# A recurrence's result kept on chip for one token group, and its square roots queued later on ScalarE

## The chip, the cores and the metric

The kernel runs on one core of one Trainium2 chip. The metric is the device time of one execution in microseconds. Before the change the median of three runs is 3213.04 us (3211.27 to 3219.51). The core has a matrix engine (TensorE, PE in the profile; PEld is its weight load), a vector engine (VectorE, DVE), an activation engine (ScalarE, ACT), GpSimd (POOL) and SyncE (SP), which here issues nearly all transfers. Each engine works through its own queue in order and meets the others through semaphores.

## The reference

One step of a hybrid decoder layer over 1024 prompt positions and 8 x 4 sample positions, 1056 rows of width 1024:

```
z  = rmsnorm(x) @ w_in
h  = x + [ rwkv7(z_r) | pool(z_p) ] @ w_out
h  = h + peer(rmsnorm(h))            # 8 heads: two scores of 128 keys, top 16 of each,
                                     # top 16 of the sums, gather of expert rows u and v
h  = h + (p @ w_ple) * sigmoid(rmsnorm(h) @ w_pg)
y  = rmsnorm(h)
```

The change lies in `rwkv7`, 8 heads of 64 with one 64 x 64 state each:

```
s    = s * w_t + (s @ -kk_t) (kk_t a_t)^T + v_t k_t^T ;   out_t = s @ r_t
out  = (out - mean(out)) * rsqrt(var(out) + 64e-5) * lnx_g + lnx_b     # per head and row
y_r  = (out + bonus) * g
```

All eight results are returned: y for both groups and the new shift, state and pooling buffers.

## The kernel before

**Stages.** Phase A projects x and makes the factors of the recurrence. Phase B is the recurrence, cut into 16 chunks of 64 prompt rows plus one for the samples. Phase C works on four token groups, columns 0 to 288, 288 to 544, 544 to 800 and 800 to 1056 (the samples are the first 32): output projection (8 blocks of `w_out`), norm, query projection (16 blocks of `wq`) and key scores. The top-k stage picks experts; for most rows it writes gates into a dense table, by one-hot matmuls or by scatters on GpSimd. Then 128 expert blocks run as dense matmuls, and the last layers follow.

**A chunk** (`bchunk`) is a generator. Each `yield` ends a turn: matmuls into one PSUM bank and a copy or product out of it. The turns are: one for `ltm` (L513), two for `lp` (L522), then an inverse by doubling, whose first copy is L533 and whose levels 1 to 5 have two turns each, a `zp` copy (L539) and a `yx` copy (L547), both on ScalarE; then `kbT` (L555), `vt` and `wn` (L560, L580), `u` (L585), the new state S on DVE (L617, L618), and the output `po`. The last part is called the tail here: head means (L625) and centring (L627) on DVE, four squarings with sums (L631), then `inv_sqrt` (a square root on ScalarE at L186 and a reciprocal on DVE at L187), a turn's end, the scaling (L634), a transposition on TensorE into a PSUM bank, two DVE products and additions into `yo` (L638, L639), and a store of `yo` to `y_d` in memory (L640, on SP). A chunk has 20 turns. Chunk c holds columns 32 + 64c onward, so chunks 8 to 11 are the third group's.

**Order.** `b_stream` keeps up to three chunks alive in three slots; a new one starts six rounds after the last at the earliest, and when a slot is free. A round gives each live chunk one turn. All chunk matmuls share one pool of four PSUM banks. Buffers such as `zp`, `yx` and `kbT` belong to a slot.

`merge` interleaves streams by shares of planned length. In step 1 phase C of the first group runs beside chunks 5 to 7; in step 2 phase C of the second beside chunks 8 to 11 and the top-k of the first; in step 3 phase C of the third beside chunks 12 to 15 and the top-k of the second; in step 4 phase C of the last with the remaining top-k and the first dense blocks. `b_stream` may run up to two chunks ahead of a step. What is traced is then put in order per engine by a planner, which simulates the engines in time and takes the ready instruction that was traced first. `tc.issue_after(l)` binds what is traced in its block to come behind `l` on `l`'s engine, in order alone and without a wait for its end.

**A group's start** (`phase_c`). The tile y is loaded from `y_d` (L720, on SP), then eight pieces of h from `hx_d` (L725), which are bound behind that load. y is split into a high and a low part (L708 on ScalarE, L709 on DVE), and the first `w_out` block follows (matmuls L677 to L679, addition to h at L739). For the two middle groups y lies in a tile `gst` of the pool `gp`, one of two buffers, which the one-hot stage also uses; the others take a tile of the work pool. The query copies on ScalarE are L800. h has one buffer; the last thing that reads it is a store (L776). Scores go to memory (L811) and come back for the top-k (L833).

Of the kernel before, what the change touches and what calls it, by code (L numbers as in the profile page):

```python
# [10 lines left out]
F32 = mybir.dt.float32  # L11
# [4 lines left out]
AF = mybir.ActivationFunctionType  # L16
# [9 lines left out]
HD = 64  # L26
# [14 lines left out]
GROUPS = ((0, 288), (288, 544), (544, 800), (800, 1056))  # L41
# [5 lines left out]
TC = 32  # L47
# [5 lines left out]
EB = 128  # L53
# [12 lines left out]
def body(ctx, tc, io):  # L66
    nc = tc.nc
    mm = nc.tensor.matmul
    TT, STT, TS, ACT = (nc.vector.tensor_tensor, nc.vector.scalar_tensor_tensor, nc.vector.tensor_scalar,
                        nc.scalar.activation)  # L70
# [7 lines left out]
    y_d = dram.tile([128, 4, T], F32, name="y_d")  # L78
# [10 lines left out]
    def v3(ap, n):  # L89
        return ap.rearrange("p (a b) -> p a b", b=n)  # L90
# [15 lines left out]
    leps_t = const.tile([128, 1], F32)  # L106
# [25 lines left out]
    def PS(tag):  # L132
        return pools[tag].tile([128, 512], F32, name="ps", tag="bc" if tag in ("b0", "b1") else tag)
# [51 lines left out]
    def inv_sqrt(out, src, scale, eps):  # L185
        ACT(out, src, AF.Sqrt, bias=eps, scale=scale)  # L186
        nc.vector.reciprocal(out, out)  # L187
# [279 lines left out]
            yield  # L467

    maxn = max(b - a for a, b in GROUPS)
    def bchunk(c, sp=None):  # L470
        smpl = sp is not None
        slot = 1 if smpl else c % NSLOT
        pst = "b0"
        tt = NSMP if smpl else 64
        pos = 0 if smpl else NSMP + 64 * c
# [3 lines left out]
        def wt(name, n, bufs=1):  # L479
            return pb.tile([128, n], F32, name=name, tag=f"{name}{slot}", bufs=bufs)  # L480

        def q4(name, bufs=1):
            return v3(wt(name, 256, bufs), 64)

        def quad(ps):
            return v3(ps[:, :256], 64)
# [4 lines left out]
        def hmm(o, l, r, start, stop):  # L491
            for hs in HS:
                mm(o[hs], l[hs], r[hs], start=start, stop=stop)  # L493

        def pmm(o, l, r, start, stop):
            for p in range(4):
                hmm(o[:, p], l[:, p], r[:, p], start and (start != "one" or p == 0), stop and (stop != "one" or p == 3))

        def turn(o, i):
            for p in range(4):  # L500
                hmm(o[:, p], i[:, p], ident2, True, True)

        f = sp[3] if smpl else pb.tile([128, 28, 64], F32, name="fdc", bufs=NSLOT + 1)
# [4 lines left out]
        ps = PS(pst)  # L508
# [6 lines left out]
        for pp in range(2):  # L515
            ps = PS(pst)
            pv = ps[:, :384].rearrange("m (i q t) -> m i q t", i=2, q=3)
            for i in range(2):
                p = 2 * pp + i
# [6 lines left out]
        yx = wt("yx", 512).rearrange("m (j q t) -> m j q t", j=2, q=4)  # L526
        Y, X = yx[:, 0], yx[:, 1]
        ps = PS(pst)
# [5 lines left out]
        for l in range(1, nlev):  # L534
            ps = PS(pst)
            hmm(ps[:, :256], id16[:, 0, :], id16.rearrange("m q t -> m (q t)"), True, False)
            pmm(quad(ps), ltm[:, l], Y, False, "one")
            zp = q4("zp")
            ACT(zp, quad(ps), AF.Copy)  # L539
            yield  # L540
            ps = PS(pst)
            n = 1 if l == nlev - 1 else 2
            pyx = ps.rearrange("m (j q t) -> m j q t", j=2, q=4)
            pmm(pyx[:, 0], X, zp, True, True)
            if n == 2:
                pmm(pyx[:, 1], zp, X, True, True)
            ACT(yx[:, :n], pyx[:, :n], AF.Copy)  # L547
            yield

        kbT = wt("kbT", 512).rearrange("m (j q t) -> m j q t", j=2, q=4)  # L550
        ps = PS(pst)
# [5 lines left out]
        ps = PS(pst)  # L557
# [41 lines left out]
        if smpl:  # L599
            po = out()  # L600
            for p in range(4):
                ps = PS(pst)
# [26 lines left out]
        s2 = wt("s2", 4)  # L629
        for p in range(4):  # L630
            STT(sq[:, p], cen[:, p], 1.0, cen[:, p], op0=ALU.mult, op1=ALU.mult, accum_out=s2[:, p:p + 1])  # L631
        inv_sqrt(s2, s2, 1.0 / HD, leps_t)
        yield
        TT(cen, cen, s2[:, :, None].to_broadcast([128, 4, 64]), op=ALU.mult)  # L634
        ps = PS(pst)
        turn(quad(ps), cen)
        yo = v3(pb.tile([128, 256], F32, name="yo", tag=f"kbT{slot}"), 64)
        TT(yo, quad(ps), fg, op=ALU.mult)  # L638
        TT(yo, yo, fo, op=ALU.add)  # L639
        nc.sync.dma_start(y_d[:, :, pos:pos + tt], yo[:, :, :tt])  # L640

    wraws = {}

    def wblock(gi, b):
        if b >= C3E and gi == NG - 1:
            hi, lo = esplit(io["wq"][b - KB])
            return [(t[0], t[1]) for t in zip(*[(x[:, :HK], x[:, HK:]) for x in (hi, lo)])]
        out = []
        for i in range(1 if b < KB else 2):
            ks = slice(i * HK, (i + 1) * HK)  # L650
            hi = ws.tile([128, HK, 128], F32R, name="whi", bufs=3)
            lo = ws.tile([128, HK, 128], F32R, name="wlo", bufs=3)
            if gi == 0:
                if b < 4:
                    raw = tk.tile([128, HK, 128], F32, name="wraw", tag="oh", bufs=2)
                else:
                    if b % 4 == 0 and i == 0:
                        wraws[0] = gp.tile([128, EB, TC], F32, name="gst", bufs=2)
                    raw = v3(wraws[0][:, 16 * (b % 4 if b < KB else 2 * (b % 4) + i):][:, :16].rearrange("p a b -> p (a b)"), 128)
                nc.sync.dma_start(raw, (io["w_out"][b] if b < KB else io["wq"][b - KB])[:, ks, :])  # L660
                ACT(hi, raw, AF.Copy)
                TT(lo, raw, hi.bitcast(F32), op=ALU.subtract)
                nc.sync.dma_start(wc_d[b, :, 0, ks, :], hi.bitcast(F32))
                nc.sync.dma_start(wc_d[b, :, 1, ks, :], lo.bitcast(F32))
            else:
                nc.sync.dma_start(hi.bitcast(F32), wc_d[b, :, 0, ks, :])
                nc.sync.dma_start(lo.bitcast(F32), wc_d[b, :, 1, ks, :])
            out.append((hi, lo))
        return out
# [23 lines left out]
    def segs(gi):  # L693
        c0, c1 = GROUPS[gi]
        if c0 == 0:
            return ((0, NP, NSMP), (NSMP, 0, c1 - NSMP))
        return ((0, c0 - NSMP, c1 - c0),)

    def tiles_of(gi):
        n = GROUPS[gi][1] - GROUPS[gi][0]  # L700
        return [(t, min(128, n - t)) for t in range(0, n, 128)]

    def phase_c(gi):
        c0, c1 = GROUPS[gi]
        n = c1 - c0
# [6 lines left out]
            ACT(hi, h[:, b, :n], AF.Copy, scale=vec(V_G2, b))  # L712
            STT(lo, h[:, b, :n], vec(V_G2, b), hi.bitcast(F32), op0=ALU.mult, op1=ALU.subtract)

        if 0 < gi < NG - 1:
            y = gp.tile([128, EB, TC], F32, name="gst", bufs=2).rearrange("p a b -> p (a b)")
            y = v3(y[:, :4 * maxn], maxn)
        else:
            y = work.tile([128, 4, maxn], F32, name="y", tag="yp")
        ly = nc.sync.dma_start(y[:, :, :n], y_d[:, :, c0:c1]).ins  # L720
        h = work.tile([128, KB, maxn], F32, name="h")
        with tc.issue_after(ly):
            for b in range(KB):
                for d, s, L in segs(gi):
                    nc.sync.dma_start(h[:, b, d:d + L], hx_d[:, b, s:s + L])  # L725
# [9 lines left out]
        for b in range(KB):  # L735
            w = wblock(gi, b)
            ps = PS("b2")
# [17 lines left out]
        a, b = max(c0, GA), min(c1, GB)  # L755
# [26 lines left out]
        for t0, m in tiles_of(gi):  # L782
            pos = c0 + t0
# [3 lines left out]
            for half in range(2):  # L787
                ps = PS("b2")
# [5 lines left out]
        for j in range(HEADS // 2):  # L794
            q = work.tile([128, 4, maxn], F32, name="q", tag="yp")
            for i in range(4):
                w = wblock(gi, KB + 4 * j + i)
                ps = PS("b2")
                mm3(ps, w, nx, n)
                l = ACT(q[:, i, :n], ps[:, :n], AF.Copy).ins  # L800
                if dn > 0 and i % 2:
                    normed(2 * j + i // 2, l)
                yield
            for t0, m in tiles_of(gi):
                ps = PS("b2")
                for i in range(4):
                    mm(ps[:m, i * 128:(i + 1) * 128], q[:, i, t0:t0 + m], keys[:, i % 2, :],
                       start=True, stop=True)
                st = tk.tile([128, 4, 128], F32, name="scs", bufs=2)
                ACT(st[:m], v3(ps[:m, :], 128), AF.Copy, scale=rt[:m, t0 // 128:t0 // 128 + 1])  # L810
                nc.sync.dma_start(sc_d[TIDX[c0 + t0], :m, 4 * j:4 * j + 4, :], st[:m])  # L811
# [226 lines left out]
    NG = len(GROUPS)  # L1038
# [51 lines left out]
    with tc.tile_pool(name="pa1", bufs=1) as pa1:  # L1090
# [4 lines left out]
        pb = pbx.enter_context(tc.tile_pool(name="pb", bufs=1, side="right", reuse_waits="tile"))  # L1095
# [99 lines left out]
    gp = gstack.enter_context(tc.tile_pool(name="gp", bufs=1))  # L1195
# [159 lines left out]
    for col in range(0, GT, 128):  # L1355
# [31 lines left out]
        for half in range(2):  # L1387
            ps = dpt.tile([128, 512], F32, name="pt")
# [149 lines left out]
    for db in range(KB):  # L1538
# [5 lines left out]
        l = tg.gate(db, w, pl, TT)  # L1544
# [5 lines left out]
    l = next(fg)  # L1550
# [77 lines left out]
```

## Time and profile before

| | |
|---|---|
| median of 3 runs | 3213.04 us |
| profiled execution | 3221.9 us, of which the span 3220.2 us |
| TensorE busy | 3048.1 us (95%) |
| weight loads busy | 2945.9 us (91%) |
| VectorE busy | 2554.8 us (79%) |
| GpSimd busy | 1702.7 us (53%) |
| ScalarE busy | 1058.8 us (33%) |
| mean granted TensorE clock | 0.972 |

The span runs from the first to the last instruction. Times in rows are microseconds from its start, unless marked ns. A row of the timeline gives start, duration, engine, line, operation, what is written from what, and in brackets how long the engine had been idle and what ended that. A row of a chain of waits gives start, duration and what was done. "q" behind an engine's name is its sequencer, which issues transfers. Buffer numbers are left out of names, so `s2` shows as `s`.

### The profile page before, as it was taken

The numbers are of one execution on the slowest core, as the hardware profiler recorded it, in microseconds if no ns is written. First come the engines' busy times: TensorE is split into PE (matmuls) and PEld (weight loads), VectorE is DVE, ScalarE is ACT, GpSimd is POOL, SyncE is SP. The second block draws the span as 40 slices with busy tenths as digits, with TensorE's granted clock in tenths as the row PEclk, the third lists the DMA queues.
The fourth block names the chain that finished last, engine by engine and source line by source line (L and its number), as shares of the span: only waits on it lengthen the run. The fifth ranks groups of instructions, "written<-read, shape, count | busy, mean of one in ns | idle before, by whom it ended". The sixth has DMA issues, their size and how long they took to land.

```text
span 3220.2 us, 65859 instructions
## 1 busy us (share of the span) xinstructions
PE 3048.1 (95%) x26305; PEld 2945.9 (91%) x26305; DVE 2554.8 (79%) x5390; ACT 1058.8 (33%) x1636; POOL 1702.7 (53%) x1189
## 2 busy tenths in 40 slices
PE   8998899978888888999999999999999999999998
PEld 7887888967777788999999999999999999999998
DVE  7766445678497888988888888888888888888976
ACT  6452324433335545322222222212222212212253
POOL 5111410077887770066666656665666666666633
PEclk9999999988989899999999999999999999999999
DMA  5577457777868987389999999999999999999945
GB/s 172 155 201 184 119 165 241 264 190 167 217 143 218 332 230 244 116 316 344 326 340 353 321 339 344 330 332 357 328 323 350 332 331 340 341 329 341 332 135 185
DMA packets 462531, 863.33 MB, mean 268 GB/s; under 512 B 152848, under 2 KB 241168, under 8 KB 461840
## 3 DMA queue, kind: packets, MB, share of 16 engines
q1 hardware_dynamic: 305776, 436.32, 42.0%
q0 software_dynamic: 148128, 406.03, 37.4%
q10 hardware_dynamic: 8320, 16.78, 1.5%
q8 instruction: 206, 3.38, 0.4%
q14 instruction: 101, 0.83, 0.1%
HBM read 738.25 MB, written 120.73 MB: 267 GB/s over the span
## 4 chain that ended last, share of the span: by engine, by line
PE 78%; DVE 9%; DMA 8%; ACT 2%; issue 1%; SPq 1%; POOL 1%; ACTq 0%; DVEq 0%; POOLq 0%
PE pd L1244 59%; PE ps L493 5%; PE ps L231 3%; PE ps L677 2%; PE ps L679 2%; PE ps L678 2%; DMA scq<-sc_d 1%; DMA whi<-wc_d 1%; PE ps L1025 1%; PE ps L324 1%; DMA wlo<-wc_d 1%; PE ps L1147 1%; DMA sc_d<-scs 1%; DVE I L837 0%; DMA y_d<-yo 0%
## 5 line engine op out<-in xcount | busy, mean ns | idle before, releaser
L1364 POOL DMA_INDIRECT row<-u,idx x384 | 545.0, 1419 | 471.7 <-DMA eraw<-uT 149.1
L1364 POOL DMA_INDIRECT row<-v,idx x384 | 530.4, 1381 | 311.6 <-DVE po L1381 141.0
L1220 ACT ACTIVATE ehi<-eraw 128x1024 fp32r<-128x1024 f32 x278 | 294.8, 1060 | 1109.0 <-PE pd L1244 1038.2
L965 POOL DMA_INDIRECT gs<-gl,idx x256 | 436.2, 1704 | 258.5 <-DVE idx L958 137.9
L1244 PE MATMUL pd<-XL,ehi 128*128 128x336 f32 x2176 | 515.6, 317 | 0.0
L1244 PE MATMUL pd<-XH,elo 128*128 128x336 f32 x2176 | 514.1, 317 | 0.0
L1244 PE MATMUL pd<-XH,ehi 128*128 128x336 f32 x2176 | 510.7, 316 | 3.0 <-ACT OT L1250 2.8
L1244 PE MATMUL pd<-wh,ehi 128*128 128x336 f32 (+1 forms) x2112 | 502.9, 317 | 4.9 <-ACT wh L1314 4.7
L1244 PE MATMUL pd<-wl,ehi 128*128 128x336 f32 (+1 forms) x2112 | 503.8, 317 | 1.7 <-DVE wl L1316 1.7
L1244 PE MATMUL pd<-wh,elo 128*128 128x336 f32 (+1 forms) x2112 | 503.4, 317 | 0.0
L1381 DVE SCALAR_TENSOR_TENSOR po<-row,act,po 128x1024 f32<-128x1024 f32 x381 | 488.1, 1281 | 7.0 <-DVE act L1375 0.2
L1372 DVE SCALAR_TENSOR_TENSOR row<-row,xt 128x1024 f32<-128x1024 f32 x384 | 455.5, 1218 | 4.9 <-DMA xt<-xt_d 3.7
L1222 DVE TENSOR_TENSOR elo<-eraw,ehi 128x1024 fp32r<-128x1024 f32 x278 | 342.7, 1233 | 85.0 <-ACT ehi L1220 84.6
L1244 PEld LDWEIGHTS pd<-XH,ehi 128*128 128x128 f32 x2176 | 372.3, 189 | 3.9 <-ACT OT L1250 3.0
L1244 PEld LDWEIGHTS pd<-XH,elo 128*128 128x128 f32 x2176 | 372.6, 188 | 0.0
L1244 PEld LDWEIGHTS pd<-XL,ehi 128*128 128x128 f32 x2176 | 370.1, 188 | 0.0
L1244 PEld LDWEIGHTS pd<-wh,ehi 128*128 128x128 f32 x2112 | 362.2, 188 | 5.5 <-ACT wh L1314 5.0
L1244 PEld LDWEIGHTS pd<-wl,ehi 128*128 128x128 f32 x2112 | 362.1, 188 | 2.0 <-DVE wl L1316 2.0
L1244 PEld LDWEIGHTS pd<-wh,elo 128*128 128x128 f32 x2112 | 363.2, 188 | 0.0
L677 PE MATMUL ps<-hi,whi 128*128 128x256 f32 (+1 forms) x592 | 188.9, 320 | 45.5 <-DMA whi<-wc_d 26.8
L1324 DVE TENSOR_TENSOR OT<-pd,OT 128x672 f32<-128x672 f32 x120 | 102.8, 857 | 136.7 <-PE pd L1244 136.3
L679 PE MATMUL ps<-hi,wlo 128*128 128x256 f32 (+1 forms) x592 | 182.7, 309 | 6.6 <-DMA wlo<-wc_d 4.8
(461 smaller groups left out, 4885.3 us busy)
## 6 DMA issues: line engine op xcount, KB each, us to landing
eraw<-uT SPq DMA_DIRECT2D x128, 512.0 KB
eraw<-vP SPq DMA_DIRECT2D x128, 512.0 KB
whi<-wc_d SPq DMA_DIRECT2D x108, 256.0 KB
wlo<-wc_d SPq DMA_DIRECT2D x108, 256.0 KB
g_d<-gst SPq DMA_DIRECT2D x52, 512.0 KB
gq<-g_d SPq DMA_DIRECT2D x32, 832.0 KB
gs<-zero ACTq DMA_DIRECT2D x8, 2048.0 KB
gq<-gs SPq DMA_DIRECT2D x64, 256.0 KB
```

The lines of the kernel that those rows point to most:

```text
L231: mm(ps[:, :XW], s[:, k, :], x[:, k, a:b], start=first, stop=last)
L493: mm(o[hs], l[hs], r[hs], start=start, stop=stop)
L677: mm(ps[:, :n], whi[:, kk, :], xhi, start=k == 0, stop=False)
L679: l = mm(ps[:, :n], wlo[:, kk, :], xhi, start=False, stop=k == K - 1)
L965: l = nc.gpsimd.indirect_dma_start(out=flat, out_offset=bass.IndirectOffsetOnAxis(ap=off[:, hh, k:k + 1], axis=0), in_=gl[:, hh, k:k + 1], ...
L1220: ACT(hi, raw, AF.Copy)
L1222: sub(lo, raw, hi.bitcast(F32), op=ALU.subtract)
L1244: mm(ps[:, a, :n], w_[:, k, :], x_[:, s:s + n], start=first, stop=last)
L1324: TT(halves(OT[db]), ps[:, :, :NH], halves(OT[db]), op=ALU.add)
L1364: nc.gpsimd.indirect_dma_start(out=r[:m], out_offset=None, in_=io[tab], in_offset=bass.IndirectOffsetOnAxis(ap=idx[:m, hh, k:k + 1], axis=0))
L1372: STT(r[:m], r[:m], 1.0, xt[:m], op0=ALU.mult, op1=ALU.mult, accum_out=pre[:m, k:k + 1])
L1381: STT(po[:m], r[:m], act[:m, k:k + 1], po[:m], op0=ALU.mult, op1=ALU.add)
```

## The change

Two things, in `bchunk` and at the head of `phase_c`.

The third group (index 2) gets its y tile when the first of its chunks reaches its tail, instead of at the start of phase C. Its four chunks write `yo` as 64-column pieces of that tile. Their stores to `y_d` and the group's load from it are left out, and the loads of h for this group are no longer bound behind that load. The other groups go through memory as before.

In every chunk's tail the square root comes three turns later, and it is bound behind the copy that was traced last by then: a `zp` or `yx` copy of any chunk, or a query copy of phase C. `lact` holds that copy.

```
+    YG, yst = 2, []
+    def ytile():
+        y = gp.tile([128, EB, TC], F32, name="gst", bufs=2).rearrange("p a b -> p (a b)")
+        return v3(y[:, :4 * maxn], maxn)
+    lact = [None]
...
-            ACT(zp, quad(ps), AF.Copy)
+            lact[0] = ACT(zp, quad(ps), AF.Copy).ins
...
-            ACT(yx[:, :n], pyx[:, :n], AF.Copy)
+            lact[0] = ACT(yx[:, :n], pyx[:, :n], AF.Copy).ins
...
-        inv_sqrt(s2, s2, 1.0 / HD, leps_t)
+        for _ in range(3):
+            yield
+        with tc.issue_after(lact[0]):
+            ACT(s2, s2, AF.Sqrt, bias=leps_t, scale=1.0 / HD)
+        nc.vector.reciprocal(s2, s2)
         yield
...
-        yo = v3(pb.tile([128, 256], F32, name="yo", tag=f"kbT{slot}"), 64)
+        here = GROUPS[YG][0] <= pos < GROUPS[YG][1] and not smpl
+        if here:
+            if not yst:
+                yst.append(ytile())
+            yo = yst[0][:, :, pos - GROUPS[YG][0]:][:, :, :64]
+        else:
+            yo = v3(pb.tile([128, 256], F32, name="yo", tag=f"kbT{slot}"), 64)
         TT(yo, quad(ps), fg, op=ALU.mult)
         TT(yo, yo, fo, op=ALU.add)
-        nc.sync.dma_start(y_d[:, :, pos:pos + tt], yo[:, :, :tt])
+        if not here:
+            nc.sync.dma_start(y_d[:, :, pos:pos + tt], yo[:, :, :tt])
...
-        if 0 < gi < NG - 1:
-            y = gp.tile([128, EB, TC], F32, name="gst", bufs=2).rearrange("p a b -> p (a b)")
-            y = v3(y[:, :4 * maxn], maxn)
+        if gi == YG:
+            y = yst[0]
+        elif 0 < gi < NG - 1:
+            y = ytile()
         else:
             y = work.tile([128, 4, maxn], F32, name="y", tag="yp")
-        ly = nc.sync.dma_start(y[:, :, :n], y_d[:, :, c0:c1]).ins
+        if gi != YG:
+            ly = nc.sync.dma_start(y[:, :, :n], y_d[:, :, c0:c1]).ins
         h = work.tile([128, KB, maxn], F32, name="h")
-        with tc.issue_after(ly):
+        with tc.issue_after(ly) if gi != YG else nullcontext():
...
-                l = ACT(q[:, i, :n], ps[:, :n], AF.Copy).ins
+                l = lact[0] = ACT(q[:, i, :n], ps[:, :n], AF.Copy).ins
```

## The prediction, made before the result was known

> **What bounds the kernel now.** I read the page first, then the busy time by stretches, then what each engine waited for in the two places that the diff touches.
>
> ```profile
> span 3220.2 us, 65859 instructions
> 343.00:501.00 158.00, 156.33 (x2674) 140.38 (x2675) 59.59 (x136) 44.22 (x104) 25.39 (x22) 0.99 0.47 147
> 669.00:870.00 201.00, 162.21 (x2544) 149.28 (x2540) 142.33 (x779) 65.43 (x146) 154.86 (x97) 0.89 0.78 184
> 870.00:1070.00 200.00, 162.06 (x2248) 148.55 (x2249) 165.30 (x749) 86.79 (x160) 161.00 (x95) 0.87 0.82 197
> 1280.00:3100.00 1820.00, 1818.96 (x11840) 1818.61 (x11841) 1589.61 (x2276) 459.11 (x552) 1091.19 (x778) 1.00 0.89 322
> ```
>
> A row of a stretch gives its length, then busy time of PE, PEld, DVE, ScalarE (ACT) and GpSimd (POOL), the granted clock, the DMA share and GB/s. From 1280 on TensorE never rests, so that part has one length and only its start can move. From 343 to 501 it rests 1.7 us. In between it rests 39 us of 201 and 38 us of 200, at clocks of 0.89 and 0.87. Nothing in this diff touches the dense part; a gain must be idle TensorE time taken away before 1280, and must not be put back before 1280.
>
> There are two such places. The first is the first chunk's tail.
>
> ```profile
> 330.00:343.00 13.00, 4.03 (x74) 3.31 (x70) 12.09 (x12) 1.02 (x4) 11.99 (x8) 0.77 0.18 61
> 331.35 8.32 DVE L631 SCALAR_TENSOR_TENSOR wn<-zp 128x64 f32<-128x64 f32 x1
> 333.78 0.68 PE L493 MATMUL ps<-zp,yx 64*64 64x64 f32 x16
> 342.36 0.30 ACT L186 ACTIVATE s<-s,leps_t 128x4 f32<-128x4 f32 x1 [11.03 <-DVE wn L631]
> 342.56 0.36 ACT L539 ACTIVATE zp<-ps 128x256 f32<-128x256 f32 x1
> 342.83 0.37 ACT L547 ACTIVATE yx<-ps 128x256 f32<-128x256 f32 x1
> 342.98 1.12 PE L493 MATMUL ps<-zp,yx 64*64 64x64 f32 x16 [8.52 <-ACT zp L539]
> ```
>
> A squaring on DVE took 8.32 us here, while GpSimd was busy 11.99 of 13 us. The square root waits for it at the head of ScalarE's queue for 11.03 us. The copies at 342.56 and 342.83 belong to other chunks and need nothing of this tail; they follow without a gap, and TensorE waits 8.52 us for the first. The group at 342.98 then takes 1.12 us where the same shape took 0.68.
>
> The second is the start of phase C for the third group.
>
> ```profile
> 855.00:872.00 17.00, 10.34 (x260) 9.55 (x256) 4.44 (x9) 6.08 (x14) 14.26 (x10) 0.92 1.06 290
> 854.61 0.53 SPq L776 DMA_DIRECT2D xl_d<-h  x1
> 856.90 0.42 DVE L639 TENSOR_TENSOR yo<-yo,fdc 128x256 f32<-128x256 f32 x1
> 857.36 5.69 DMA y_d<-yo
> 863.11 6.78 DMA gst<-y_d
> 863.78 6.45 SPq L725 DMA_DIRECT2D h<-hx_d  x8
> 870.27 0.91 SPq L833 DMA_DIRECT2D scq<-sc_d  x2
> 869.91 1.34 ACT L708 ACTIVATE hi<-gst 128x256 fp32r<-128x256 f32 x4 [6.84 <-DMA gst<-y_d]
> ```
>
> Chunk 11's result is done on DVE at 857.32. It goes to memory (5.69 us) and comes back (6.78 us); the first split of y stands at 869.91. SP's queue holds the loads of h and of the next scores behind the load of y. So TensorE rests 6.7 of 17 us and DVE 12.6.
>
> **The change, part by part.** *The round trip.* Four stores of 128 rows and one load leave SP and the DMA queues; the eight loads of h lose their order behind that load. The result is added into the group's tile by the same two DVE instructions. If chunk 11's tail stayed where it is, the split could follow at 857.4 instead of 869.91: 12.5 us, the upper bound of this part.
>
> By the Trainium skill ("DMA: Bandwidth & Descriptors", Anatomy of one DMA), a transfer takes some 2.0 us and its bytes at 436 GB/s, given there for GpSimd-issued ones. By that page 128 KiB and 512 KiB take an estimated 2.3 and 3.2 us, so the removed trip would be 5.5 us and the sum below about 7 us poorer, near -5. The trace does not agree: 5.69 and 6.78 us, at a DMA share of 1.06 in that stretch.
>
> *The later square root.* The tail now gives up its turn three times more, and the root is queued behind the last copy traced by then. A round is one turn of every live chunk, so one copy per chunk. Counting rounds from the code, chunk 0's root goes behind chunk 2's third-level yx copy, chunk 7's behind chunk 9's third-level yx, and chunk 11's behind chunk 13's first zp. A chunk lives 23 turns instead of 20; with three slots, one starts every 7.7 rounds instead of 6.7, and chunk 13, which takes chunk 10's slot, starts three rounds later against chunk 11.
>
> At 331 to 343 the copies of two other chunks can now go. A hop costs TensorE one or two groups of 16 matmuls, 0.68 us each warm, so three rounds of two chunks, six hops, are about 5 us of work pulled into the rest. The slow clock after it adds 0.44 us a group (1.12 for 0.68), some 2 us over the first four or five. Bounds: 0, if the anchor copy comes before 342 with nothing behind it, and 8.5 + 2 = 10.5. I take **7 us**, since TensorE rests only 1.7 us of the next 158, so that work pulled forward shortens them.
>
> Chunk 11's tail does get later, and that is charged against the 12.5.
>
> ```profile
> 803.40 0.30 ACT L186 ACTIVATE s<-s,leps_t 128x4 f32<-128x4 f32 x1 [4.48 <-DVE wn L631]
> 806.18 0.42 DVE L639 TENSOR_TENSOR yo<-yo,fdc 128x256 f32<-128x256 f32 x1
> 843.70 0.30 ACT L186 ACTIVATE s<-s,leps_t 128x4 f32<-128x4 f32 x1 [8.84 <-DVE wn L631]
> 852.99 0.38 ACT L539 ACTIVATE zp<-ps 128x256 f32<-128x256 f32 x1 [3.15 <-PE ps L493]
> 856.04 0.60 ACT L547 ACTIVATE yx<-ps 128x512 f32<-128x512 f32 x1 [1.56 <-PE ps L493]
> 861.48 0.38 ACT L580 ACTIVATE wn<-ps 128x256 f32<-128x256 f32 x1 [1.25 <-PE ps L493]
> ```
>
> The copy at 852.99 is chunk 13's first zp, 9.3 us behind the root at 843.70. If it keeps its time, the root at 853.4 and 3.2 us from root to result (803.40 to 806.60) give 856.6: nothing lost. With chunk 13 three rounds later it falls into the round of chunk 12's wn copy, 861.48; the root then stands at 861.9, the result at 865.1, the split at 865.4, and 4.5 of the 12.5 us are left. The code's order speaks for the later one, so I take **5 us** of gain, from bounds of 0 (the rounds stay slow) and 12.5.
>
> At the second group nothing is taken out and the tail is later as well.
>
> ```profile
> 646.33 0.30 ACT L186 ACTIVATE s<-s,leps_t 128x4 f32<-128x4 f32 x1 [2.71 <-DVE wn L631]
> 652.05 0.48 DVE L639 TENSOR_TENSOR yo<-yo,fdc 128x256 f32<-128x256 f32 x1
> 653.72 9.07 DMA y_d<-yo
> 662.81 5.86 DMA gst<-y_d
> 656.51 0.38 ACT L539 ACTIVATE zp<-ps 128x256 f32<-128x256 f32 x1
> 666.52 0.68 ACT L810 ACTIVATE scs<-ps,rt 32x512 f32<-32x512 f32 x1 [7.58 <-DMA sc_d<-scs]
> 667.10 0.57 ACT L547 ACTIVATE yx<-ps 128x512 f32<-128x512 f32 x1
> 668.69 1.34 ACT L708 ACTIVATE hi<-gst 128x256 fp32r<-128x256 f32 x4 [1.02 <-DMA gst<-y_d]
> ```
>
> Chunk 9's third yx stands at 667.10, held by a copy that waits for a store; without that, the zp at 656.51 and the 3 us from a zp to its yx (852.99 to 856.04) would put it near 659.5. The root moves from 646.33 to between 660 and 667.7, the result from 652.5 to between 663 and 671. With a transfer of 5.69 us instead of 9.07, phase C of the second group starts 7 to 15 us later. SP, DVE's scan and the recurrence do not need y and can go on. That group's last query copy stands at 853.41, so it ends at 860 to 868 instead of 853; chunk 11's tail is at 865 then, by the paragraph above. The two end together, so I charge **nothing** beyond the 5 us. If the covers fail, it is 10 us (the bound above). The reason to believe in the cover is DVE: it is done with chunk 7 at 652.5 and busy 142 of the next stage's 201 us with a scan that can start without y.
>
> Inside the second stage the root also held other copies.
>
> ```profile
> L186 ACT ACTIVATE s<-s,leps_t 128x4 f32<-128x4 f32 x17 | 5.1, 297 | 51.8 <-DVE wn L631 51.8
> 703.04 0.41 DVE L639 TENSOR_TENSOR yo<-yo,fdc 128x256 f32<-128x256 f32 x1
> 743.01 0.30 ACT L186 ACTIVATE s<-s,leps_t 128x4 f32<-128x4 f32 x1 [6.62 <-DVE wn L631]
> 743.21 0.36 ACT L533 ACTIVATE yx<-ps 128x256 f32<-128x256 f32 x1
> ```
>
> The 17 roots idled ScalarE for 51.8 us; 8.84 of them, at 843.70, held nothing up. In the stage of chunks 8 to 11 the two that did are 6.62 and 4.48, together 11.1 us returned at most. Against them stands the longer life: chunks 8 to 11 finish 51 us apart (703.0 to 856.9 in three steps), 7.7 us a round, and each costs a round more. I take **0** between -11 and +19 (the first rival).
>
> The held tile costs nothing: it is one of two buffers that the one-hot stage uses too, and counting allocations in order, the next stage tile falls into the other. If it did not, that stage would wait for the split, which ends near 871 in the row above.
>
> Sum: -7 - 5 = **-12 us**. The profiled execution took 3221.9 us, 1.7 us around its span, and would take 3209.9. It stands 8.9 us above the median of 3213.04; from the median, **3201 us**.
>
> **The rivals.** *Rounds set the pace (slower).* Place: the stage 669 to 870. PSUM banks go round in the order traced, so a round lasts as long as its slowest hop and the idle turns of a tail are not free. Four chunks times one round of 7.7 us is 31 us: chunk 11's result at 888 instead of 857.3, the split at 888.4 instead of 869.91, +19, with the 7 us of the start +12: 3225 us. It decides once chunk 11's result comes after some 877. For it: 51 us between results is 20 turns over three slots. Against it: DVE and ScalarE waits, 11.1 us here, are part of those rounds.
>
> *Phase C waits for h anyway (no change).* h's one buffer is freed by the store issued at 854.61, and its eight loads took 6.45 us to issue. If they land as before, the third group starts no earlier and only the 7 us remain: 3206 us. Against it: the loads were queued behind y.
>
> *The root still blocks (no change).* If the planner sets the root straight behind its anchor and that copy runs before the squares are done, ScalarE waits as before; the diff then does not do what it says. Left is the 5 us at 870: 3208 us.
>
> *All of it (faster still).* Chunk 13's copy keeps 853, giving 12.5 us; the 10.5 us at 343 come in full, and a few of the 11.1: -26, 3187 us.
>
> ```profile
> 1198.24 2.96 POOL L965 DMA_INDIRECT gs<-gl,idx  x1 [0.30 <-issue]
> 1268.33 0.92 SPq L1308 DMA_DIRECT2D gq<-gs  x2
> ```
>
> That the scatters on GpSimd cap any gain is no rival: the last starts at 1198.24 and is first read at 1268.33, 67 us after its end.
>
> **How the numbers follow.** Forecast 0.38, slower rounds 0.22, h 0.16, blocking root 0.10, all of it 0.14. About 0.3% (9.6 us) is what a measurement here can tell from no change. The forecast's own range is 3193 to 3207, so 0.08 of its 0.38 falls within 0.3%. Faster: 0.30 + 0.14 = 0.44; same: 0.08 + 0.16 + 0.10 = 0.34; slower: 0.22. With both signs in it, the range runs from all of it to the slower rival, 3186 to 3226.
>
> **What would show it.** Right: no rest of TensorE over 4 us near 335; the third group's first split within 1 us of chunk 11's last addition, some 8 to 12 us earlier than 869.91 once the start's gain is in; roots without idle time before them. Wrong: results of chunks 8 to 11 some 59 us apart; the second group's split more than 12 us late and its last query copy as late; the third group's first addition to h as late as before although its split is early; or a TensorE rest before 1280 longer by what was taken out.

## The result, and the profile after

The change makes the kernel slower. Its median is 3227.5 us (3222.09 to 3241.45, 11 runs) against 3213.04 us for the kernel before (11 runs beside it); the ratio is 1.0055, interval 1.0042 to 1.0068, some 13 to 22 us. The forecast was 3201 us, faster. The profiled execution took 3232.6 us.

First the page's head and the busy time by stretches of the kernel after, in the columns of the prediction. Then come three longer stretches ahead of the dense part, for the kernel before and, in the last fence, for the one after.

```profile
span 3230.9 us, 65827 instructions
330.00:343.00 13.00, 8.44 (x176) 8.05 (x172) 11.02 (x11) 2.35 (x5) 10.55 (x7) 0.83 0.21 62
343.00:501.00 158.00, 153.68 (x2579) 138.22 (x2575) 60.01 (x137) 43.16 (x101) 25.53 (x22) 0.98 0.46 145
1280.00:3100.00 1820.00, 1820.00 (x11879) 1819.96 (x11878) 1589.69 (x2297) 461.33 (x556) 1095.05 (x776) 1.00 0.90 322
```

```profile
300.00:600.00 300.00, 280.55 (x5078) 254.88 (x5072) 142.31 (x331) 103.58 (x240) 51.94 (x45) 0.97 0.60 189
600.00:850.00 250.00, 208.54 (x3166) 192.64 (x3163) 180.54 (x975) 89.92 (x193) 158.63 (x99) 0.90 0.77 198
850.00:1100.00 250.00, 199.60 (x2730) 181.66 (x2729) 192.49 (x785) 111.41 (x194) 198.90 (x116) 0.86 0.88 223
```

```profile
300.00:600.00 300.00, 285.46 (x5123) 259.89 (x5119) 142.99 (x333) 106.27 (x242) 50.47 (x43) 0.98 0.61 192
600.00:850.00 250.00, 207.84 (x3131) 191.60 (x3130) 176.55 (x968) 87.93 (x190) 161.54 (x102) 0.90 0.76 195
850.00:1100.00 250.00, 188.93 (x2661) 171.04 (x2659) 195.71 (x791) 108.40 (x187) 196.08 (x115) 0.86 0.82 201
```

The dense stretch is full before and after, so the time lies ahead of it. Up to 600 us TensorE rests 14.5 us instead of 19.5: five are gained. From 850 to 1100 it rests 61.1 us instead of 50.4: more than ten are lost. From 1100 to 1300 two more are lost.

**The roots block nothing any more.** The group of the 17 roots on ScalarE, whose idle time was 51.8 us:

```profile
L643 ACT ACTIVATE s<-s,leps_t 128x4 f32<-128x4 f32 x17 | 5.0, 291 | 0.1
```

**The starts of the three later groups.** Rows of the timeline after, with the two transfers of the second group from the chain of waits.

```profile
674.79 0.41 DVE L657 TENSOR_TENSOR yo<-yo,fdc 128x256 f32<-128x256 f32 x1
675.23 2.31 DMA y_d<-yo
677.56 5.71 DMA gst<-y_d
683.29 1.03 ACT L727 ACTIVATE hi<-gst 128x256 fp32r<-128x256 f32 x3 [5.67 <-DMA gst<-y_d]
...
849.06 0.38 ACT L821 ACTIVATE q<-ps 128x256 f32<-128x256 f32 x1 [4.76 <-PE ps L698]
...
856.92 0.30 ACT L643 ACTIVATE s<-s,leps_t 128x4 f32<-128x4 f32 x1
869.60 0.40 DVE L657 TENSOR_TENSOR gst<-gst,fdc 128x256 f32<-128x256 f32 x1
870.03 1.33 ACT L727 ACTIVATE hi<-gst 128x256 fp32r<-128x256 f32 x4 [11.10 <-DVE gst L657]
...
1056.29 0.38 ACT L821 ACTIVATE q<-ps 128x256 f32<-128x256 f32 x1 [0.89 <-PE ps L698]
1056.77 0.29 ACT L643 ACTIVATE s<-s,leps_t 128x4 f32<-128x4 f32 x1
1066.42 0.42 DVE L657 TENSOR_TENSOR yo<-yo,fdc 128x256 f32<-128x256 f32 x1
1092.48 0.57 SPq L741 DMA_DIRECT2D y<-y_d  x1
1100.19 1.33 ACT L727 ACTIVATE hi<-y 128x256 fp32r<-128x256 f32 x4 [7.56 <-DMA y<-y_d]
```

The second group's first split stands at 683.3 instead of 668.7, its last query copy at 849.1 instead of 853.4. The third group's split starts 0.4 us after the start of chunk 11's last addition, without a trip through memory. But that addition comes 12.7 us later (869.6 for 856.9), and the split is where it was: 870.03 for 869.91.

What held chunk 11's result shows in four rows of TensorE and VectorE between the root at 856.92 and the split:

```profile
858.07 0.65 PE L501 MATMUL ps<-ident,zp 64*64 64x64 f32 x16
865.95 0.87 DVE L857 MAX8 V<-scq 128x8 f32<-128x128 f32 x4 [8.06 <-DMA scq<-sc_d]
868.05 0.41 DVE L656 TENSOR_TENSOR gst<-ps,fdc 128x256 f32<-128x256 f32 x1
870.50 0.58 PE L696 MATMUL ps<-hi,whi 128*128 128x256 f32 x1 [8.88 <-ACT hi L727]
```

The transposition, which is all that the product at L656 needs of the tail, is over at 858.7, 1.8 us after the root. The product starts 9.3 us later. Ahead of it in VectorE's queue stands a top-k instruction of the second group (`MAX8`), which waits 8.06 us for its scores from memory; then some 2 us of top-k run first. TensorE rests 8.88 us until the split. So the root no longer blocks ScalarE here, but its result waits behind another blocked instruction, on VectorE. A `MAX8` waits in the same place, ahead of chunk 11's product, for 6.5, 8.9 and 6.1 us in e2, e3 and e13 below. No run here puts the products ahead of it.

The last group starts 19 us later. Chunk 15's root stands behind a query copy of the third group, and on SP the load of y now stands behind sixteen loads of XH and XL. The kernel before had, for the last two rows of the three starts:

```profile
1069.94 0.57 SPq L720 DMA_DIRECT2D y<-y_d  x1
...
1081.12 1.04 ACT L708 ACTIVATE hi<-y 128x256 fp32r<-128x256 f32 x3
```

**What releases the dense stretch.** Two things stand last ahead of it in the chain: the last one-hot comparison of the third group on VectorE (`ab<-iota,e`), whose product goes to memory and returns as gates, and the last query copy of the last group on ScalarE. The timelines before (first two rows) and after:

```profile
1245.77 1.20 DVE L1017 TENSOR_TENSOR ab<-iota,e 128x2048 f16<-128x2048 f16 x1
1260.02 0.36 ACT L800 ACTIVATE q<-ps 128x256 f32<-128x256 f32 x1
```

```profile
1238.26 1.23 DVE L1038 TENSOR_TENSOR ab<-iota,e 128x2048 f16<-128x2048 f16 x1 [1.17 <-PE ps L1046]
1284.77 0.38 ACT L821 ACTIVATE q<-ps 128x256 f32<-128x256 f32 x1 [1.59 <-PE ps L698]
```

Over all 18 profiles of this study the span is the larger of (that comparison + 1974.3) and (that copy + 1946): within 0.7 us in ten of them, off by 1.7 to 5.5 in the other eight. Six of the ten are the profiles that the constants were taken from; of the twelve later ones four fit. By this rule the comparison decides before (1245.8 + 1974.3 = 3220.1); after, the comparison comes earlier and the copy decides (1284.8 + 1946 = 3230.8). The rule describes; that one of the two causes the end is argued from the chain and not shown.

### The profile page after: what moved, and what is told of

It is laid out like the page before. It is cut to its first block, busy times and chain, and to the rows that moved or that the text cites. A ratio compares the mean times of both kernels' runs of the same rounds, so it can differ in the third digit from the quotient of the medians.

```text
span 3230.9 us, 65827 instructions
## 1 busy us (share of the span) xinstructions
PE 3049.7 (94%) x26305; PEld 2947.2 (91%) x26305; DVE 2553.8 (79%) x5390; ACT 1059.1 (33%) x1636; POOL 1703.1 (53%) x1189
## 4 chain that ended last, share of the span: by engine, by line
PE 80%; DVE 8%; DMA 7%; ACT 2%; SPq 1%; issue 1%; POOL 1%; ACTq 0%; DVEq 0%; POOLq 0%
PE pd L1265 60%; PE ps L501 5%; PE ps L231 3%; PE ps L696 2%; PE ps L698 2%; PE ps L697 2%; DMA whi<-wc_d 1%; DMA wlo<-wc_d 1%; DMA sc_d<-scs 1%; PE ps L324 1%; DMA scq<-sc_d 1%; PE ps L1046 1%; PE ps L1168 1%; ACT gst L1047 1%; PE ps L828 0%
## 5 line engine op out<-in xcount | busy, mean ns | idle before, releaser
L986 POOL DMA_INDIRECT gs<-gl,idx x256 | 428.6, 1674 | 256.8 <-DVE idx L979 136.7
```

The lines of the kernel that those rows point to most:

```text
L986: l = nc.gpsimd.indirect_dma_start(out=flat, out_offset=bass.IndirectOffsetOnAxis(ap=off[:, hh, k:k + 1], axis=0), in_=gl[:, hh, k:k + 1], ...
```

## The experiments

All medians, ratios and ends in one table. "One-hot" and "copy" are the starts of those two instructions in the profile; the profiled execution is often some us off the median. Each ratio is to the kernel before on the same chip. The runs were spread over three chips, so kernels are compared by their ratios.

| kernel | median us | ratio to before, interval | one-hot | copy | span |
|---|---|---|---|---|---|
| the change | 3227.5 | 1.0055 (1.0042 to 1.0068) | 1238.3 | 1284.8 | 3230.9 |
| e1 y tile alone | 3229.7 | 1.0054 (1.0033 to 1.0075) | 1246.1 | 1238.4 | 3219.9 |
| e1b the same again | 3235.9 | 1.0079 (1.0053 to 1.0106) | 1261.4 | 1253.7 | 3233.4 |
| e2 late roots alone | 3226.8 | 1.0048 (1.0032 to 1.0063) | 1238.5 | 1283.0 | 3228.9 |
| e3 change, root 15 early | 3224.2 | 1.0036 (1.0024 to 1.0047) | 1242.7 | 1254.5 | 3217.6 |
| e5 root 15 late alone | 3214.5 | 1.0002 (0.9991 to 1.0014) | 1236.6 | 1250.9 | 3210.7 |
| e10 tile and memory | 3210.8 | 0.9995 (0.9980 to 1.0009) | 1242.4 | 1256.7 | 3216.3 |
| e13 late but 15 | 3220.3 | 1.0026 (1.0011 to 1.0040) | 1230.0 | 1270.9 | 3216.8 |
| e14 tile, last group held | 3222.9 | 1.0044 (1.0025 to 1.0064) | 1229.1 | 1271.1 | 3217.4 |
| e16 first five late | 3200.0 | 0.9965 (0.9953 to 0.9977) | 1226.0 | 1236.0 | 3197.5 |
| e21 late but 7, 11, 13 to 15 | 3206.6 | 0.9984 (0.9975 to 0.9994) | 1237.3 | 1242.8 | 3206.3 |
| e22 root 7 late alone | 3240.4 | 1.0085 (1.0066 to 1.0103) | 1275.8 | 1261.0 | 3247.0 |
| e6 turns, no binding | 3217.1 | 1.0018 (1.0008 to 1.0029) | 1239.1 | 1240.9 | 3215.1 |
| e24 late but 7, 15 | 3210.9 | 1.0001 (0.9991 to 1.0011) | 1220.4 | 1251.6 | 3200.5 |
| e23 change, root 7 early | 3226.7 | 1.0051 (1.0033 to 1.0069) | 1255.6 | 1260.9 | 3224.4 |
| e25 tile, first five late | 3183.4 | 0.9916 (0.9897 to 0.9935) | 1205.9 | 1231.5 | 3182.8 |
| e26 root 6 late alone | 3205.9 | 0.9989 (0.9974 to 1.0003) | 1215.6 | 1255.8 | 3202.4 |

### The halves, and the last tail

e1 leaves the root where it was; e2 leaves y in memory; e3 is the change with chunk 15's root in its old place; e5 has only that root late.

```
e1   here = GROUPS[YG][0] <= pos < GROUPS[YG][1] and not smpl ; inv_sqrt as before
e2   here = False ; late root in every chunk
e3   the change, with:  if c < 15: (late root)  else: inv_sqrt(...)
e5   here = False ; if c == 15: (late root)  else: inv_sqrt(...)
```

> The third group's tile is kept on chip, the square roots stay where they were. Last-tail theory (the loss is chunk 15's root, queued behind a query copy of the third group): faster than before by 6 to 12 us, ratio 0.996 to 0.998, the third group's first split within 1 us of chunk 11's last addition and before 862. Slow-rounds theory (three turns more per chunk set the pace): also faster, 5 to 12 us, since the turns are as before. Tile theory (the held tile or the freed loads of h do the harm): slower by 10 us or more, ratio 1.003 or above.

> The roots come three turns later and behind the last copy, y goes through memory for all groups. Last-tail and slow-rounds theories: slower than the changed kernel, by the round trip that comes back, so ratio to before 1.006 to 1.011, third group's split near 882. Tile theory: as fast as before, ratio 0.997 to 1.001.

> The changed kernel, but chunk 15's root alone keeps its old place (no turns more, not bound). Last-tail theory: the loss goes, ratio to before 0.995 to 1.001, the last group's first split back near 1081 to 1087 and the first dense matmul back near 1075. Slow-rounds theory: the loss stays, ratio 1.004 or above, since sixteen of seventeen tails still hold their slots three turns longer.

> The kernel before, but chunk 15's root alone comes three turns later and behind the last copy (a query copy of the third group). Last-tail theory: slower by 8 to 20 us, ratio 1.0025 to 1.006, chunk 15's result some 15 to 20 us later than 1045.7, the last group's split and the first dense matmul later with it. Slow-rounds theory: no change, ratio 0.999 to 1.001, since one chunk's turns at the end hold no slot that anyone waits for.

Each half alone costs about what the whole costs, so the parts do not add. In e1 only the tile theory's forecast came true; e2 lies below what two theories named and above the third. Putting chunk 15's root back returns a third of the loss (e3, 1.0036 for 1.0055, though the intervals overlap a little), so the last tail is not the whole cause, as the first theory had it. e5 says nothing on a late last group: there the root was bound behind a query copy at 1015.9 while its squares were done only at 1026, so it was not delayed and chunk 15's result came at 1038.7, ahead of the 1045.7 of before.

### The y tile by itself

e10 takes the tile as early as the change does and writes the pieces there, but stores them to memory too and loads them back into the same tile. e14 is e1 with chunk 15's root twelve turns later, behind a later query copy. e1b is e1 again.

```
e10  -        if not here:
     -            nc.sync.dma_start(y_d[...], yo[...])
     +        nc.sync.dma_start(y_d[...], yo[...])          # and the load into yst[0]
e14  if c == NCH - 1: for _ in range(12): yield ; (late root)  else: inv_sqrt(...)
```

> The y tile alone once more, unchanged, because its first profile (span 3219.9 us) lay 8 us below its median and only four executions stand behind it. Six profiles so far (before, after, the tile alone, the late roots alone, all roots but the last late with the tile, the last root alone) fit one rule within 0.5 us: the span is the larger of (start of the third group's last one-hot comparison on VectorE, plus 1974.3) and (start of the last group's last query copy, plus 1946). Two-ends theory: this profile fits that rule again, with the one-hot as the larger term, and if the span is near 3228 the last comparison starts near 1254. Rival, the loss lies in the dense part: the comparison starts near 1246 as before and the span is 3228 all the same. Time: 3222 to 3231.

> The y tile is taken as early as in the change and its pieces are written there, but the four stores to memory and the load back into the same tile stay, and h stays bound behind that load; the roots are as before. So the tile's buffer is held for the same time and nothing starts earlier. Holding theory (one of the two one-hot buffers is missing from chunk 8's tail to the group's start): as slow as the y tile alone, 3224 to 3231. Early-start theory (the loss comes from the third group's earlier start, which brings the last group's projections into the queues ahead of the third group's one-hots): no change, 3208 to 3218, third group's first split near 870.

> The y tile alone, and chunk 15's root put behind the third group's query copy 14, so that the last group starts some 13 us later than with the tile alone (first split near 1085 instead of 1072). Early-start theory: the last group's projections then stand behind more of the third group's one-hots; the last comparison starts near 1240 instead of 1246 to 1254 and the time comes back by 6 to 14 us, to 3214 to 3222. Rival, any later work is later at the end: the time grows by up to 13 us, to 3230 to 3242. If the start of the last group has no part in it, the time is that of the tile alone.

The tile costs nothing while it is held (e10, 0.9995). What costs is what e10 puts back: it restores the trip, and with it the later start (split at 869.1) and the order of the loads of h, which no run tells apart. Whether holding the last group back returns a part is not settled: e14 stands at 1.0044 against 1.0079 for e1b on the same chip, but the intervals overlap, and e1 on another chip had 1.0054. So on the kernel before, the y tile with its earlier third group is a loss; that the earlier start is the reason is likely and not separated from the rest. In e1b the rule above gave the right order, with the comparison later than the 1254 expected, and missed the span by 2.3 us.

One place where the third group runs differently is its output projection. The rows are the waits from that group's start to its first query copy, over 62 to 80 us: first e1, then the kernel before, then e25 and e16, which are described below. A row gives who waited for whom, us in total, times and the longest.

```profile
ACT sq L758 <- DVE h L756: 23.3, 6, 8.8
```

```profile
ACT sq L741 <- DVE h L739: 7.2, 5, 2.1
```

```profile
ACT sq L765 <- DVE h L763: 11.4, 5, 3.3
```

```profile
ACT sq L763 <- DVE h L761: 5.5, 5, 1.9
```

And in e1's timeline and busy time:

```profile
873.18 0.42 ACT L758 ACTIVATE sq<-h 128x256 f32<-128x256 f32 x1 [8.79 <-DVE h L756]
873.50 0.49 ACT L727 ACTIVATE hi<-h,vecs 128x256 fp32r<-128x256 f32 x1
873.90 0.58 ACT L555 ACTIVATE yx<-ps 128x512 f32<-128x512 f32 x1
870.00:890.00 20.00, 12.49 (x167) 11.18 (x164) 20.00 (x150) 4.48 (x12) 16.45 (x12) 0.74 0.56 106
```

This is the pattern of the root at 342, in another place. A square of phase C stands at the head of ScalarE's queue for 8.79 us, because the addition to h is queued on VectorE (20.00 busy of 20) among the second group's top-k; a recurrence copy goes straight after it. The third group starts 21 us earlier in e1 (848.6 for 869.9), but its last query copy is only 8 us earlier (1055.0 for 1063.4). In e1b it starts 13 us earlier (857.0), and that copy is 4 us later (1067.2). That this wait is the cause of the loss is not shown: from 600 to 1280 us it adds up to 39.3 us in e1 for 33.2 before, and to only 17.0 in the change, which is as slow; and with the tile it doubles from e16 to e25, though the time falls.

### Which late roots cost

e13 has every root late but chunk 15's; e24 also leaves 7 early, e21 also 11, 13 and 14; e16 has only chunks 0 to 4 and the samples late. e22 and e26 have one late root each. e6 keeps the three turns in every chunk but does not bind the root. In all of these y goes through memory.

```
e13  if c < NCH - 1:                      (late root)  else: inv_sqrt(...)
e24  if c not in (7, NCH - 1):
e21  if c not in (7, 11, 13, 14, 15):
e16  if c < 5:
e22  if c == 7:
e26  if c == 6:
e6   for _ in range(3): yield ; inv_sqrt(s2, s2, 1.0 / HD, leps_t)
```

> All roots late but chunk 15's, y through memory as before. Two-ends theory: the late roots alone lost through the last group's last query copy (1283 us, 1946 to the end: 3229); with chunk 15's result back near 1037 that copy comes near 1255 and the third group's one-hots decide again, near 1238 plus 1974: 3209 to 3216, no change. Rival, the later start of the second group costs by itself (600 to 900: TensorE rests 60 us instead of 54): 3219 to 3226.

> Only the roots of chunks 0 to 4 and of the samples are late; y goes through memory, the other roots stay. Between 300 and 600 us TensorE rests 19 to 20 us in the three profiles with early roots and 12.5 to 16.6 in the four with late ones, so some 5 us are gained there. Theory that the gain travels on to the third group's one-hots: 3204 to 3209. Rival, that it is absorbed before the third group's last query copy: 3210 to 3215.

> The roots of chunks 0 to 6, 8 to 10, 12 and the samples are late; those of 7 and 11 (the last of the second and third group) and of 13 to 15 (which would wait for a query copy) stay early; y goes through memory. Theory that a late root costs only where a group's start waits for it: as with the first five late or better, 3202 to 3210, second group's first split near 668. Rival, the longer life of every chunk costs: 3216 to 3224.

> Only chunk 7's root is late, behind chunk 9's third-level yx copy as in the change, so only the second group starts later (first split near 678 to 684 instead of 668). If that start is covered, as the prediction had it: 3208 to 3216, second group's last query copy within 3 us of 853. Rival, it costs what TensorE rests more between 600 and 900 (7 to 9 us): 3219 to 3224.

> The three turns before the root in every chunk, without the binding behind a copy; y through memory. Two-ends theory: chunk 15's root no longer waits for the third group's query copy 13, its result comes 10 to 18 us earlier than with the bound roots (1063), the last group's last query copy near 1265 to 1272 instead of 1283, and 3211 to 3219. Rival, the longer life alone costs: 3224 to 3230 as with the bound roots.

> All roots late but chunk 7's and chunk 15's; y through memory. All but chunk 15's measured 3220.3 us, and with 7, 11, 13 and 14 early as well it was 3206.6. Theory that chunk 7's root, which the second group's start waits for, is the cost: 3203 to 3211. Rival, that chunks 11, 13 and 14 carry it: 3216 to 3224.

> Only chunk 6's root late; no group starts on chunk 6. Theory that chunk 7's root costs because the second group's start waits for it: 3208 to 3216. Rival, that any single late root there costs through another order of the queues: 3225 or more.

The late roots form a ladder. All late: 1.0048. Without 15: 1.0026. Without 7 as well: 1.0001. Without 11, 13 and 14 as well: 0.9984. The first five and the samples alone: 0.9965. Each step down returns about 0.2%, with intervals that touch or overlap those of the next, so a single step is barely clear of noise; the ladder as a whole is clear. By it the late roots of chunks 5 to 15 cost 0.8%, no single step carries the loss, and the useful part of the edit is its first third. The binding matters too: with the turns alone the loss is 1.0018 (e6). e6's time fell in the range that was named, but its copy stood at 1240.9 and not at 1265 to 1272, so the reason given for it did not hold. e13 came out as its rival had it, with the copy at 1270.9; e16 is faster than either theory; e21 and e24 fell where their first theories had them.

Of the roots tried alone, chunk 7's is the dearest: 28 us (21 to 33), more than either expectation, against no measurable difference for chunk 6 (e26). In e22 the second group's split stands at 686 and its queries do not catch up as they do in the change:

```profile
860.88 0.38 ACT L822 ACTIVATE q<-ps 128x256 f32<-128x256 f32 x1 [5.72 <-PE ps L701]
...
1076.51 0.38 ACT L822 ACTIVATE q<-ps 128x256 f32<-128x256 f32 x1 [2.20 <-PE ps L701]
...
1275.81 1.21 DVE L1039 TENSOR_TENSOR ab<-iota,e 128x2048 f16<-128x2048 f16 x1
```

The last query copies of the second and third group are 7.5 and 13 us later than before, the last one-hot comparison 30 us. Why 17 us at the start become 28 at the end, and why chunks 8 to 11 with late roots shrink that, is not settled.

### What is left of the change

e23 is the change with chunk 7's root early; e25 is the y tile with the first five roots late.

```
e23  the change, with:  if c != 7: (late root)  else: inv_sqrt(...)
e25  the change, with:  if c < 5:  (late root)  else: inv_sqrt(...)
```

> The whole change, but chunk 7's root in its old place. If the second group's start is the larger part of the change's loss: 3210 to 3220, second group's first split near 666. If the last group's start (chunk 15's root behind a query copy) holds the end whatever came before: 3223 to 3231, with the last query copy plus 1946 as the span.

> Late roots of chunks 0 to 4 and the samples (3200.0 us by themselves) and the y tile. Early-start theory (the third group's earlier start costs by what it brings ahead of the one-hots): 3212 to 3226, third group's first split near 832 instead of 844. Rival, the tile's loss hung on the old order of that stage alone: 3194 to 3204.

With 7 early the change is as slow as with 7 late (1.0051 for 1.0055), but not by the mechanism expected: of the rule's two terms the one-hots are the larger (1255.6), not the copy, and the rule is 5.5 us off here. e25 beats both kernels: 0.9916, some 21 to 33 us faster than before, and faster than either expectation. Its timeline at the third group, and the stretch from 600 to 850:

```profile
832.12 0.42 DVE L660 TENSOR_TENSOR gst<-gst,fdc 128x256 f32<-128x256 f32 x1
832.57 1.34 ACT L730 ACTIVATE hi<-gst 128x256 fp32r<-128x256 f32 x4 [0.73 <-DVE gst L660]
600.00:850.00 250.00, 220.07 (x3428) 201.55 (x3428) 183.61 (x987) 94.82 (x212) 157.57 (x98) 0.94 0.84 221
```

In e16, which keeps the trip, the chain of waits has for the same place:

```profile
830.71 5.78 DMA y_d<-yo
836.55 7.66 DMA gst<-y_d
```

So the trip takes 13.4 us here, much as in the rows of before (5.69 and 6.78 us). The estimate of 5.5 us worked out from the Trainium skill ("DMA: Bandwidth & Descriptors", Anatomy of one DMA) is overruled by the measurement. The split comes 11.7 us earlier in e25 than in e16 (832.57 for 844.24). In the stretch from 600 to 850 TensorE rests 29.9 us in e25, 33.1 in e16 and 41.5 in the kernel before, so most of that gain is the late roots', and 3 us the tile's. So my theory after e14, that the earlier third group costs by itself, falls: the same tile that costs 0.5 to 0.8% on the kernel before gains 0.5% on e16. Why the additions to h stand behind the top-k in e1 and less so in e25 is open; both start the third group 4 us after the second group's last query copy.

## Why the prediction was wrong

Three steps failed: the path (an earlier third group was taken to end the kernel earlier), one term of the third group's sum (3.2 us from root to result, measured 12.7), and the price of the late roots behind chunk 4 (0 or none, by the ladder 0.8%). They are shown in pieces; how much of the loss each carries in the change itself stays open, since the pieces do not add.

- **The dense stretch has one length.** Right: 1820.00 us busy of 1820. But I followed no chain up to its start; I assumed that rest taken away anywhere before 1280 moves it. By the rule both kernels are released by work of the third or last group, and the five us gained up to 600 are gone by then.
- **Chunk 0's root, -7.** Right in sign, as the first part of a ladder: chunks 0 to 4 and the samples are worth 12 us (e16). At 330 to 343 TensorE works 8.44 us for 4.03. VectorE's slow instruction did not go away, though (see below): TensorE still waits 4.6 us in one piece for the centring behind it, where I had named 4 us as the most.
- **The second group, "nothing".** Its split came 14.6 us later, the top of my 7 to 15, and its last query copy 4 us earlier; by that test the cover held. In the change, chunk 7's root back in its old place returns nothing that can be measured (e23). Yet the same root alone costs 28 us, and taking it out of e13 returns 8. So the charge of nothing is not refuted for this kernel, but a group's last copy was the wrong place to look for the cost.
- **The third group, -5.** This step failed in one term: 3.2 us from root to result, taken from chunk 10 (803.40 to 806.60). Chunk 13's copy came 3.7 us later than before and not in the later round (root at 856.92, not 861.9), so by my own 3.2 us the result was due at 860.1; it came at 870.0. What I left out is VectorE's queue: the transposition was done at 858.7, and the product stood behind a `MAX8` that waited for scores. That the root-to-result time of chunk 11 before was nearly as long (843.70 to 857.32) is a coincidence and explains nothing here: there the transposition itself came late on TensorE (855.76), behind blocks of phase C. The 12.5 us of the trip were used up.
- **The path.** The bound of 12.5 us took for granted that an earlier split is a gain. In e1 the split comes 21 us earlier, more than that bound, and the kernel is 0.5% slower; on e16 the same tile gains 0.5%.
- **Roots 13 to 15.** I priced three roots of seventeen. Chunk 15's went behind a query copy, which no paragraph names; the last group starts 19 us later and its last copy comes 25 us later. e13 against e2, and e3 against the change, both give 0.2% for it.
- **The rounds, 0.** Right in their length: chunks 8 to 11 finish 50.9 us apart (716.9 to 869.6 in three steps) for 51.3 before. That the late roots cost nothing there is not shown: with those of chunks 5, 6, 8 to 10 and 12 the ratio goes from 0.9965 (e16) to 0.9984 (e21). The slower rival named 3225 us, near the measured time, but by longer rounds, 59 us apart; its mechanism did not occur. The blocking root did not occur either: 0.1 us of idle time for 51.8.
- **The wait for h, as a rival.** In the change it did not occur: the loads of h are issued from 856.8 to 860.8, before the split. In e1 and e25, where the split comes early, VectorE's first addition does wait 5.9 us for h.
- **The held tile, 0.** Right (e10).
- **The sum.** Terms from four places were added as if each moved the end by itself. The tile is worth +0.5% or -0.5% by what stands beside it, so no sum of single terms could have held.

## What to carry to other kernels

Before pricing a saving, follow the chain back from the start of the part that never rests, and ask of each edit whether it moves that releaser. Where an edit is repeated over a loop, price each place by its own rows, the last iterations before a hand-over above all, and put it only where something waits behind it: of the sets tried here, six of seventeen roots, those of chunks 0 to 4 and the samples, did best. An operation that waits at the head of an in-order queue is worth moving, but starting other work earlier can put the next such operation there. So follow the moved work through every queue that it still has to pass: chunk 11's root was free of ScalarE's queue and then stood in VectorE's.

## What the runs showed of the hardware that was not expected

**A victim, not a culprit.** In the kernel before, a squaring on VectorE took 8.32 us at 331. After the change the squarings are short (1.46 and 0.21 us), and the addition to the state was the long one. VectorE and GpSimd after:

```profile
328.35 10.01 DVE L626 TENSOR_TENSOR S<-S,pcs 128x256 f32<-128x256 f32 x1
328.59 4.82 POOL L130 TENSOR_TENSOR plo<-pT,phi 128x1056 fp32r<-128x1056 f32 x2
333.35 2.51 POOL L130 TENSOR_TENSOR apb<-spf,cmask 128x512 f32<-128x512 f32 x2
335.80 1.26 POOL L130 TENSOR_TENSOR wlo<-wraw,whi 128x512 fp32r<-128x512 f32 x1
337.01 1.06 POOL L1181 CAST yhi<-yraw 128x1056 fp32r<-128x1056 f32 x1
```

The same addition (L618 there) took 0.60 us before. It ended at 338.36, 0.3 us after the last of these GpSimd rows, which follow each other without a gap; the next GpSimd instruction stands at 338.15. The Trainium skill ("SBUF — State Buffer", SBUF: two separate sides) says that VectorE and GpSimd share a port pair as an exclusive lock, held for a whole instruction; the trace agrees in that the wait is whole, and shows it across several GpSimd instructions in a row. The addition's row begins 0.24 us before the first of them, so which came first can't be read from it, and no run takes the GpSimd work away to show that it is the cause. In nine of the kernels here one VectorE instruction of this place is long, 6.0 us (e1) to 10.0 us: a squaring in e2 (7.46 us) and e25 (8.09 us), the addition in e16 (9.43 us). The victim changes, and the wait stays.

**The same program, profiled twice.** e1 and e1b are one program; their spans are 3219.9 and 3233.4 us. Between 800 and 900 us TensorE was busy 81.3 and 81.9 of 100, at granted clocks of 0.93 and 0.83. A difference of 10 us between two single profiles of this kernel is therefore no evidence without the medians beside it, and that holds for the columns "one-hot" and "copy" above too.
